# Split products with the weights' low part last, states in 2 KB runs, and small conversions on ScalarE, in a one-core decoder step

## The chip, the cores and the metric

The kernel runs on one core of a Trainium2 chip. The metric is the time of one execution on the device in microseconds, the median over several runs. Besides, one execution was recorded by the hardware profiler; its rows carry the names of the engines: PE (TensorE, matrix products), PEld (its weight loads), DVE (VectorE), ACT (ScalarE), POOL (GpSimd) and SP (SyncE, which here only issues DMAs). "SPq" and "ACTq" are the instructions that issue DMAs on those queues.

## The reference

One layer of a decoder, in float32, for 1024 prompt tokens and 64 sample tokens (8 sequences of 8), width 1024. Cut to what matters:

```python
xn = rmsnorm(h, norm_mix)
proj = xn @ w_in                      # 2048 columns for retention, 1792 for RWKV-7
# retention, 8 heads of 64: q, k with rope, state S (64 x 64) per sequence and head, chunks of 128
o_ret = head_norm(retention(q, k, v, s_ret)) * silu(g_ret)
# RWKV-7, 8 heads of 64: f mixes each row with the row before it (token shift)
f = rw_p + (prev - rw_p) * rw_mu
o_rw = (head_norm(rwkv7_scan(r, log_w, k7, kk, a, v7, s_wkv)) ... ) * gate
h = h + concat([o_ret, o_rw]) @ w_out
# PEER: product keys, 8 heads x 2 x 128 keys, 16 of 16384 experts for each head and token
s = einsum(xb @ wq, keys); sv, si = top_k(s, 16)
cand = sv[:, :, 0, :, None] + sv[:, :, 1, None, :]; cv, ci = top_k(cand, 16)
e = si0[ci // 16] * 128 + si1[ci % 16]
act = gelu(einsum('pd,phkd->phk', xb, u_tab[e])) * softmax(cv)
h = h + einsum('phk,phkd->pd', act, v_tab[e])
h = h + sigmoid(rmsnorm(h, ple_norm) @ ple_gate) * (p_l @ ple_proj)
y = rmsnorm(h, norm_final)
```

Returned besides `y` are the new states of both mixers for the prompt and for each of the 8 sequences of the sample group, and the last projected rows.

## The kernel before

Tokens are tiled by 128: tiles 0 to 7 are the prompt, tile 8 holds the 64 sample tokens.

**Split products.** A product that needs more than one pass's precision is made from two parts of each operand. `split` (L296) has ACT copy the source into the high part (type float32r), and DVE or POOL subtract that from the source for the low part. `mm3` (L324) then adds three products for each step k of the contraction: high by high, high by low, low by high. It is called for the projections (`a_ret`, L361, with the tokens as the stationary operand and the weights `wh`, `wl` moving; `a_rw`, L519, with the weights stationary), for the queries (`c_query`, L1006), for `hidden` (L1259, the weights `uh`, `ul` stationary, eight steps) and for `ple` (L1376, the tokens stationary). `dense` (L1288) has the same three products written out, for blocks b of 128 experts: `vh` by `ah`, `vh` by `al`, `vl` by `ah`.

**Stages.** In order of time:

1. Projections (`group_a`, three groups of tiles: 0 and 1, 2 and 3, 4 to 8). Results go to DRAM: `rd` for retention and `fd` for RWKV. `fd` is one tensor of 128 partitions x 14 x 1088 tokens; `a_rw` writes one of the 14 rows for all tokens of its group at a time (L559), on ACT's queue.
2. Mixers (`group_b`, L648), tile by tile in the order 1, 8, 2 to 7. `rw_mix` loads its tile's part of `fd` into `ft` (L708, one buffer). Tile 8 reads and writes the states of the eight sequences: `seq_state` (L422) for both mixers, L489 and L493 for retention, L947 and L955 for RWKV. In DRAM a state is laid out sequence, head, row, column, so that each of 64 partitions takes eight pieces of 64 values. Behind the mixers run `c_rows` (the output projection, with its weights `cw` loaded on SP's queue) and the expert search and gathers of tiles 0, 1 and 8 (`early`, L1214).
3. Queries and first top 16 of the tiles 2 to 7 (`c_query`, `pick`).
4. `topk` (L1041) for tiles 4 to 7 (group `G2`) and 2 and 3 (`G1`), the gates of G2 (`gates`, L1230: one-hot matrices, scaled by ACT at L1247, multiplied on PE), and `hidden` for the first 96 blocks of 128 experts, whose results are stored in DRAM (`gd`).
5. For G2 all 16384 experts are computed densely: `dense_fused` (L1310) for the last 32 blocks, in groups of four, with `hidden` for the next group between; then `dense_stored` (L1329) for the 96 stored blocks in groups of five. For each group `act` (L1273) makes `ah` and `al` from eight buffers (`AB`); then for each of eight slices d of the width, `dense` loads `vraw`, splits it (`vh` on ACT, `vl` on POOL, two buffers each), runs the products of the group into one PSUM tile `py`, and adds that to `yT` on DVE (L1307).
6. `ple`: the last gate, the final norm and the output.

**Gathers.** For G1 the experts are fetched row by row (`gather`, L1120): POOL issues an indirect DMA of 128 rows of 4 KB (L1130) into one of five buffers, and DVE multiplies and sums each (L1144 for `u`, L1158 for `v`). They run beside stages 4 and 5, on the same POOL and DVE queues as the splits of the weights and the sums into `yT`.

**Order.** Each engine runs its instructions in one fixed order. The kernel is built with `TileContext(nc, schedule_with_timeline_sim=True)`: the order in each queue is planned when the program is built, from a simulated time line, not taken as written. Waits follow from the tiles' readers and writers and from their buffers.

**Conversions.** In `topk`, DVE turns the found indices from integers to floats (L1053) and scales half of them by 128 (L1054), turns the second search's indices into floats (L1079), and for G2 the two halves of the expert's number (L1118). In `gates`, DVE copies the transposed softmax out of PSUM (L1237).

Of the kernel before, what the change touches and what calls it, by code (L numbers as in the profile page):

```python
# [8 lines left out]
F32 = mybir.dt.float32  # L9
# [4 lines left out]
AF = mybir.ActivationFunctionType  # L14
# [10 lines left out]
RW = 1792  # L25
# [89 lines left out]
def pack(i):  # L115
    f = lambda a: np.asarray(a)
    w_in = f(i['w_in'])[0]
    r = {}
    r['x'] = np.concatenate([f(i['x_prompt'])[0], f(i['x_sample']).reshape(64, D)], 0)
    r['w_ret'] = w_in[:, :RET].reshape(8, 128, 8, 256).transpose(2, 1, 0, 3)  # L120
    r['w_rw'] = w_in[:, RET:].reshape(8, 128, 14, 128).transpose(2, 1, 0, 3)
    r['w_out'] = f(i['w_out'])[0].reshape(8, 128, 1024)
    col = lambda a, n: a.reshape(n, 128).T
    r['vec'] = np.concatenate([col(f(i['rw_mu'])[0], 14), col(f(i['rw_kk'])[0], 4), col(f(i['rw_ka'])[0], 4),
                               col(f(i['rw_rk'])[0].reshape(512), 4), col(f(i['rw_a0'])[0], 4)], 1)
    r['w2aug'] = np.concatenate([f(i['rw_w2'])[0], f(i['rw_w0'])], 0)
    r['a2'] = f(i['rw_a2'])[0]
    r['g2'] = f(i['rw_g2'])[0]
    r['rows'] = np.concatenate([f(i['norm_mix'])[0], f(i['norm_ffn'])[0], f(i['ple_norm'])[0], f(i['norm_final']),
                                f(i['rw_ln_g'])[0], f(i['rw_ln_b'])[0]])  # L130
    r['s_ret'] = f(i['state_ret'])[0]
    r['s_wkvT'] = f(i['state_wkv'])[0].transpose(0, 1, 3, 2)
    r['shiftT'] = f(i['state_shift'])[0].reshape(8, 14, 128).transpose(2, 1, 0)
    r['cst'] = consts()
    r['rope'] = ropes()
    r['wq'] = f(i['peer_wq'])[0].reshape(8, 128, 16, 128).transpose(2, 1, 0, 3)
    r['keysT'] = f(i['peer_keys'])[0].reshape(16, 128, 128).transpose(2, 0, 1)
    r['pu'] = f(i['peer_u'])[0]
    r['puT'] = r['pu'].reshape(128, 128, 8, 128).transpose(0, 3, 2, 1)
    r['pv'] = f(i['peer_v'])[0]  # L140
    r['pvd'] = r['pv'].reshape(128, 128, 8, 128).transpose(2, 1, 0, 3)
    p = np.concatenate([f(i['p_prompt'])[0, 0], f(i['p_sample'])[0].reshape(64, 256)], 0)
    r['pT'] = p.T.reshape(2, 128, T).transpose(1, 0, 2)
    r['pgate'] = f(i['ple_gate'])[0].reshape(8, 128, 1024)
    r['pproj'] = f(i['ple_proj'])[0].reshape(2, 128, 1024)
    return {k: np.ascontiguousarray(v) for k, v in r.items()}


OUTS = {'y': ((T, D), 'float32'), 'ret_p': ((8, 64, 64), 'float32'), 'wkv_p': ((8, 64, 64), 'float32'),
        'shift': ((9, RW), 'float32'), 'ret_s': ((8, 8, 64, 64), 'float32'), 'wkv_s': ((8, 8, 64, 64), 'float32')}  # L150
ROWS = {'norm_mix': (0, 1024), 'norm_ffn': (1024, 1024), 'ple_norm': (2048, 1024), 'norm_final': (3072, 1024),
# [3 lines left out]
def unpack(r):  # L155
    return (r['y'][:SEQ].reshape(1, SEQ, D), r['y'][SEQ:].reshape(8, 8, D),
            r['ret_p'].reshape(1, 1, 8, 64, 64), r['wkv_p'].reshape(1, 1, 8, 64, 64), r['shift'][:1].reshape(1, 1, RW),
            r['ret_s'].reshape(1, 8, 8, 64, 64), r['wkv_s'].reshape(1, 8, 8, 64, 64), r['shift'][1:].reshape(1, 8, RW))

# [53 lines left out]
class K:  # L213
# [28 lines left out]
    def setup(self):  # L242
        nc = self.nc
        rp = self.pool("root")
        self.dp = self.pool("dscr", space=bass.MemoryType.DRAM)
        self.csta = rp.tile([128, CSTA], F32, name="csta")
        nc.sync.dma_start(self.csta, self.I['cst'][:, :CSTA])
        self.hp = rp.tile([128, 8], F32, name="halves")
        nc.vector.memset(self.hp, -0.5)
        self.eid = {t: rp.tile([128, 64 if t == 8 else 128], I32, name=f"eid{t}") for t in E0 + G1}  # L250
        self.gsm = {t: rp.tile([128, 64 if t == 8 else 128], F32, name=f"gsm{t}") for t in E0 + G1}
        self.hd = {t: self.dp.tile([128, D], F32, name=f"hd{t}") for t in range(9)}
        self.xd = {t: self.dp.tile([128, D], F32, name=f"xd{t}") for t in range(9)}
        self.od = {t: self.dp.tile([128, D], F32, name=f"od{t}") for t in range(9)}
        self.yd = {t: self.dp.tile([128, D], F32, name=f"yd{t}") for t in range(9)}
        self.fd = self.dp.tile([128, 14, T], F32, name="fd")
        self.sd = {t: self.dp.tile([128, 16, 128], F32, name=f"sd{t}") for t in range(9)}
        self.rd = {t: self.dp.tile([128, RET], F32, name=f"rd{t}") for t in range(9)}
# [64 lines left out]

    def mm3(self, out, lh, ll, rh, rl, nk, first=True, last=True):  # L324
        mm = self.nc.tensor.matmul
        for k in range(nk):
            mm(out, lh(k), rh(k), start=first and k == 0, stop=False)  # L327
            mm(out, lh(k), rl(k), start=False, stop=False)  # L328
            mm(out, ll(k), rh(k), start=False, stop=last and k == nk - 1)  # L329

# [30 lines left out]
    def a_ret(self, wp, tiles, x, ready, tags):  # L361
        nc, I = self.nc, self.I
        off, _ = spans(tiles)
        if True:
            for cb in range(8):
# [10 lines left out]
                for t in tiles:  # L376
# [3 lines left out]
                    self.mm3(p[:n, :256], lambda k: x[0][:, k, o:o + n], lambda k: x[1][:, k, o:o + n],  # L380
                             lambda k: wh[k // 4][:, k % 4, :], lambda k: wl[k // 4][:, k % 4, :], 8)
                    d = wp.tile([128, 256], F32, name="retd", bufs=4)
# [39 lines left out]
    def seq_state(self, wp, src, st, hp):  # L422

        nc = self.nc
        sr = wp.tile([128, 8, 64], F32, name="sr", tag="x2k", bufs=CRING)
        for s in range(2):
            nc.sync.dma_start(sr[64 * s:64 * s + 64], st[:, 2 * hp + s].rearrange("b j i -> j b i"))
        return wp, src, sr
# [9 lines left out]
    def ret_mix(self, wp, t):  # L438
# [41 lines left out]
        if smp:  # L480
            stk = self.c("seqtok", 64)
            for h in range(8):
# [5 lines left out]
                s0 = self.co.tile([64, 8, 64], F32, name="sr0", tag="x2k", bufs=4)  # L488
                nc.sync.dma_start(s0, I['s_ret'][:, h].rearrange("b d v -> d b v"))  # L489
                sn = self.co.tile([64, 8, 64], F32, name="srn", tag="x2k", bufs=4)  # L490
                nc.vector.tensor_tensor(sn, p[:64].rearrange("p (b d) -> p b d", b=8), s0, op=OP.add)
                nc.vector.tensor_scalar(sn, sn, self.c("gc8", 64)[:, h:h + 1], None, op0=OP.mult)
                nc.scalar.dma_start(O['ret_s'][:, h].rearrange("b d v -> d b v"), sn)  # L493
                yield
# [24 lines left out]
    def a_rw(self, wp, tiles, x, tags):  # L519
# [6 lines left out]
        for i, ft in enumerate((12, 13, 4, 5, 6, 7, 0, 1, 2, 3, 8, 9, 10, 11)):  # L526
# [27 lines left out]
            if smp:  # L554
# [3 lines left out]
                nc.vector.tensor_copy(self.shl[:, 1:9, ft], rs[:, :, 8])  # L558
            nc.scalar.dma_start(self.fd[:, ft, t0:t0 + ntok], dst)  # L559
        if smp:  # L560
# [135 lines left out]
    def rw_mix(self, t):  # L696
# [10 lines left out]
        ft = wp.tile([128, 14, n], F32, name="ft")  # L707
        nc.sync.dma_start(ft, self.fd[:, :, o:o + n])  # L708
        rT, kT, vT = ft[:, 0:4, :n], ft[:, 4:8, :n], ft[:, 8:12, :n]
# [222 lines left out]
        else:  # L932
# [6 lines left out]
            for h in range(8):  # L939
# [6 lines left out]
                s0 = self.co.tile([64, 8, 64], F32, name="sw0", tag="x2k", bufs=4)  # L946
                nc.sync.dma_start(s0, I['s_wkvT'][:, h].rearrange("b j i -> j b i"))  # L947
                nc.vector.tensor_tensor(s0, p[:64].rearrange("p (b d) -> p b d", b=8), s0, op=OP.add)
# [5 lines left out]
                nc.scalar.activation(s1, p2[:64], AF.Copy)  # L954
                nc.scalar.dma_start(O['wkv_s'][:, h].rearrange("b i j -> i b j"), s1)  # L955
                yield
# [84 lines left out]
    def topk(self, tp, t, s=None, tags={}, ce=None):  # L1041
# [10 lines left out]
        sf = tp.tile([128, 8, 2, 16], F32, name="sf")  # L1052
        nc.vector.tensor_copy(sf[:n].rearrange("p h c k -> p (h c) k"), si[:n])  # L1053
        nc.vector.tensor_scalar(sf[:n, :, 0], sf[:n, :, 0], 128.0, None, op0=OP.mult)  # L1054
        svv = sv.rearrange("p (h c) k -> p h c k", c=2)
# [22 lines left out]
        cf = tp.tile([128, 128], F32, name="cf")  # L1078
        nc.vector.tensor_copy(cf[:n], ci[:n].rearrange("p h k -> p (h k)"))  # L1079
        ef = tp.tile([128, 128], F32, name="ef")  # L1080
# [31 lines left out]
        else:  # L1112
# [4 lines left out]
            nc.vector.tensor_scalar(e1[:n, 1], ei[:n], 127, None, op0=OP.bitwise_and)  # L1117
            nc.vector.tensor_copy(self.e12[t][:n], e1[:n])  # L1118

# [110 lines left out]
    def gates(self, wp, t):  # L1230
# [5 lines left out]
        it = wp.tile([128, 128], F32, name="it", bufs=2)  # L1236
        nc.vector.tensor_copy(it[:, :n], p[:, 2, :n])  # L1237
        io = self.c("iota")[:, None, :].to_broadcast([128, 4, 128])
# [49 lines left out]
    def dense(self, dl, dr, yT, groups, acts_of, side):  # L1288
        nc, I = self.nc, self.I
        for g0, nb in groups:  # L1290
            acts = acts_of(g0, nb)
            for d in range(8):
# [6 lines left out]
                p = self.ps2.tile([128, self.ntok], F32, name="py")  # L1299
                for b in range(nb):  # L1300
                    ah, al = acts[b]
                    for j, (lh, rh) in enumerate(((vh, ah), (vh, al), (vl, ah))):
                        nc.tensor.matmul(p, lh[:, b, :], rh, start=b == 0 and j == 0, stop=b == nb - 1 and j == 2)  # L1303
                if self.first:
# [253 lines left out]
```

## Time and profile before

| | |
|---|---|
| median of 3 runs | 3877.64 us (3877.34 to 3881.52) |
| profiled execution, its own time | 3881.51 us |
| its span, first to last instruction | 3879.7 us |
| mean granted clock of PE | 0.883 |
| PE busy | 3346.4 us (86%) |
| DVE busy | 2984.9 us (77%) |
| POOL busy | 2361.5 us (61%) |
| ACT busy | 1220.5 us (31%) |
| moved by DMA | 1086.23 MB, mean 280 GB/s |

The span is the profiled execution's time but for 1.8 us around it. A busy time is a sum over the whole span; the stages differ much, so that no share of the table is the share of a stage. A row of a group names the line, the engine, the operation and the tiles written and read; a row of a wait names who waited, who ended the wait, the total in us, how often, and the longest one.

### The profile page before, as it was taken

What the parts mean: (1) busy time and instruction counts of PE and PEld (TensorE: products, weight loads), DVE (VectorE), ACT (ScalarE), POOL (GpSimd) and SP (SyncE); (2) the same over time, 40 slices, a digit from 0 to 9 for tenths busy, and PEclk for the clock granted to TensorE, in tenths of its full rate; (3) what the DMA queues carried; (4) which work ended last, traced back from release to release, by engine and by line L of the source; (5) the groups of instructions that cost most, each with busy time, mean ns of one, the idle gap of its engine ahead of it and who ended that gap; (6) DMA issues with size and microseconds to landing.
All of it is one profiled execution on the core that took longest, in us unless ns stands there. A gap on an engine that the chain in (4) does not pass through costs nothing.

```text
span 3879.7 us, 52665 instructions
## 1 busy us (share of the span) xinstructions
PE 3346.4 (86%) x17749; PEld 2748.3 (71%) x17749; DVE 2984.9 (77%) x5884; ACT 1220.5 (31%) x2247; POOL 2361.5 (61%) x2059
## 2 busy tenths in 40 slices
PE   7789995868779878883999989999899989899979
PEld 7688894645747757662887767887688766677757
DVE  4454388877787697876998999977777777788875
ACT  4232220111111111211232626777533333333322
POOL 5363176454365365554569888875688787777740
PEclk9799995667868567876999999999899999999989
DMA  7266558899778878889779888998999999999962
GB/s 249 74 218 208 172 179 285 279 300 296 231 243 285 294 264 272 290 288 327 223 261 309 298 289 316 315 349 320 346 339 339 336 361 359 358 352 345 334 223 72
DMA packets 457320, 1086.23 MB, mean 280 GB/s; under 512 B 73627, under 2 KB 176281, under 8 KB 452378
## 3 DMA queue, kind: packets, MB, share of 16 engines
q0 software_dynamic: 165888, 604.05, 44.4%
q1 hardware_dynamic: 236638, 382.77, 31.0%
q10 hardware_dynamic: 54524, 96.03, 6.6%
q8 instruction: 141, 2.31, 0.2%
q14 instruction: 129, 1.06, 0.1%
HBM read 986.68 MB, written 95.94 MB: 279 GB/s over the span
## 4 chain that ended last, share of the span: by engine, by line
PE 37%; DVE 24%; DMA 12%; POOL 8%; issue 8%; ACT 3%; ACTq 0%; SPq 0%; POOLq 0%; DVEq 0%
PE py L1303 13%; DVE grow L1144 6%; POOL grow L1130 4%; DMA grow<-in_pu,eid 4%; DVE gacc L1158 3%; DMA grow<-in_pv,eid 3%; PE ph L327 2%; PE ph L329 2%; PE ph L328 2%; POOL vl L302 2%; PE epq L1198 2%; DMA ft<-fd 2%; DVE eq L1085 2%; PE ewo L612 2%; DVE oh L1245 1%
## 5 line engine op out<-in xcount | busy, mean ns | idle before, releaser
L1130 POOL DMA_INDIRECT grow<-in_pv,eid x576 | 572.0, 993 | 497.4 <-DVE gacc L1158 310.2
L1130 POOL DMA_INDIRECT grow<-in_pu,eid x576 | 573.3, 995 | 432.5 <-DVE grow L1144 257.9
L1158 DVE SCALAR_TENSOR_TENSOR gacc<-grow,ac,gacc 128x1024 f32<-128x1024 f32 x571 | 732.2, 1282 | 51.1 <-DMA grow<-in_pv,eid 46.3
L1144 DVE SCALAR_TENSOR_TENSOR grow<-grow,gacc 128x1024 f32<-128x1024 f32 x576 | 690.3, 1213 | 87.8 <-DMA grow<-in_pu,eid 77.2
L1303 PE MATMUL py<-ah,vl 128*128 128x512 f32 x1024 | 410.0, 403 | 40.6 <-POOL vl L302 40.0
L1303 PE MATMUL py<-ah,vh 128*128 128x512 f32 x1024 | 406.9, 398 | 16.1 <-ACT vh L298 9.5
L329 PE MATMUL ph<-cx,ul 128*128 128x512 f32 x1024 | 406.5, 398 | 14.4 <-POOL ul L302 14.3
L327 PE MATMUL ph<-cx,uh 128*128 128x512 f32 x1024 | 408.6, 399 | 5.4 <-ACT uh L298 3.6
L328 PE MATMUL ph<-cx,uh 128*128 128x512 f32 x1024 | 406.2, 397 | 0.0
L1303 PE MATMUL py<-al,vh 128*128 128x512 f32 x1024 | 405.0, 396 | 0.0
L302 POOL TENSOR_TENSOR vl<-vraw,vh 128x640 fp32r<-128x640 f32 (+2 forms) x224 | 325.5, 1457 | 33.3 <-ACT vh L298 29.6
L302 POOL TENSOR_TENSOR ul<-uraw,uh 128x1024 fp32r<-128x1024 f32 x128 | 308.0, 2406 | 53.5 <-ACT uh L298 50.9
L1303 PEld LDWEIGHTS py<-ah,vl 128*128 128x128 f32 x1024 | 193.4, 189 | 108.0 <-POOL vl L302 67.0
L298 ACT ACTIVATE vh<-vraw 128x640 fp32r<-128x640 f32 (+2 forms) x224 | 154.5, 692 | 356.4 <-PE py L1303 173.8
L1307 DVE TENSOR_TENSOR yT<-yT,py 128x512 f32<-128x512 f32 x216 | 147.7, 685 | 127.7 <-PE py L1303 126.9
L1303 PEld LDWEIGHTS py<-ah,vh 128*128 128x128 f32 x1024 | 194.5, 190 | 69.2 <-ACT vh L298 21.9
L329 PEld LDWEIGHTS ph<-cx,ul 128*128 128x128 f32 x1024 | 194.7, 190 | 60.6 <-POOL ul L302 20.9
L327 PEld LDWEIGHTS ph<-cx,uh 128*128 128x128 f32 x1024 | 194.9, 190 | 46.7 <-ACT uh L298 5.3
L298 ACT ACTIVATE uh<-uraw 128x1024 fp32r<-128x1024 f32 x128 | 135.2, 1057 | 286.9 <-DMA uraw<-in_puT 144.3
L1303 PEld LDWEIGHTS py<-al,vh 128*128 128x128 f32 x1024 | 193.8, 189 | 44.2
L328 PEld LDWEIGHTS ph<-cx,uh 128*128 128x128 f32 x1024 | 195.3, 191 | 39.3
L1245 DVE TENSOR_TENSOR oh<-csta,pit 128x512 f32<-128x512 f32 x256 | 162.3, 679 | 43.1 <-PE pwt L1250 42.9
(400 smaller groups left out, 7806.7 us busy)
## 6 DMA issues: line engine op xcount, KB each, us to landing
uraw<-in_puT SPq DMA_DIRECT2D x128, 512.0 KB, 4.7
vraw<-in_pvd SPq DMA_DIRECT2D x152, 320.0 KB, 5.9
cw<-in_w_out SPq DMA_DIRECT2D x128, 256.0 KB, 5.2
wd<-wst ACTq DMA_DIRECT2D x28, 1024.0 KB, 15.2
wt<-wd SPq DMA_DIRECT2D x64, 448.0 KB, 7.6
wraw<-in_w_ret SPq DMA_DIRECT2D x48, 512.0 KB, 4.9
ewq<-in_wq SPq DMA_DIRECT2D x48, 512.0 KB, 5.1
gd<-geh ACTq DMA_DIRECT2D x96, 256.0 KB, 5.2
```

The lines of the kernel that those rows point to most:

```text
L298: nc.scalar.activation(hi, src, AF.Copy)
L302: nc.gpsimd.tensor_tensor(lo, src, hi.bitcast(F32), op=OP.subtract)
L327: mm(out, lh(k), rh(k), start=first and k == 0, stop=False)
L328: mm(out, lh(k), rl(k), start=False, stop=False)
L329: mm(out, ll(k), rh(k), start=False, stop=last and k == nk - 1)
L612: nc.tensor.matmul(p[:n], oT[k // 4][:, k % 4, :n], w, start=k == 0, stop=k == 7)
L1130: nc.gpsimd.indirect_dma_start(out=g, out_offset=None, in_=src, in_offset=bass.IndirectOffsetOnAxis(ap=self.eid[t][:, j:j + 1], axis=0))
L1144: nc.vector.scalar_tensor_tensor(g[:, c], g[:, c], 1.0, x[:, c], op0=OP.mult, op1=OP.mult, accum_out=hv[:, i, j:j + 1])
L1158: nc.vector.scalar_tensor_tensor(y[:, c], g[:, c], ac[:, j:j + 1], y[:, c], op0=OP.mult, op1=OP.add)
L1245: nc.vector.tensor_tensor(oh[j], io, p[:, j, s + b:s + b + 4, None].to_broadcast([128, 4, 128]), op=OP.is_equal)
L1303: nc.tensor.matmul(p, lh[:, b, :], rh, start=b == 0 and j == 0, stop=b == nb - 1 and j == 2)
L1307: nc.vector.tensor_tensor(yT[:, d, :], yT[:, d, :], p, op=OP.add)
```

## The change

Five edits. The computation stays the same; sums are added in another order.

- In `mm3` and in `dense`, the products of a group that use the low part of the stationary operand come after all others, in a second loop. `a_ret`, where the weights are the moving operand, passes `right=True`, which puts the products with the moving operand's low part last instead. `ple` doesn't pass it.
- The states of the sample group lie in DRAM as head, row, sequence, column, in the inputs and the outputs, so that a partition's eight pieces are one run of 2 KB instead of eight of 256 bytes. The host turns them before and after.
- `fd` lies as tile, partition, row, token, so that a tile's load is one run of 7 KB in each partition. The stores are cut at tiles into runs of 512 bytes, and the sample tokens get a store of their own.
- In `topk`, for the tiles 2 to 7, the conversion of the indices (L1053 and L1054 become two instructions), of the second search's indices (L1079), and of the halves (L1118) go to ACT.
- In `gates`, the copy L1237 goes to ACT.

```diff
-        self.fd = self.dp.tile([128, 14, T], F32, name="fd")
+        self.fd = self.dp.tile([9, 128, 14, 128], F32, name="fd")
...
-    def mm3(self, out, lh, ll, rh, rl, nk, first=True, last=True):
+    def mm3(self, out, lh, ll, rh, rl, nk, first=True, last=True, right=False):
         mm = self.nc.tensor.matmul
         for k in range(nk):
             mm(out, lh(k), rh(k), start=first and k == 0, stop=False)
-            mm(out, lh(k), rl(k), start=False, stop=False)
-            mm(out, ll(k), rh(k), start=False, stop=last and k == nk - 1)
+            mm(out, *((ll(k), rh(k)) if right else (lh(k), rl(k))), start=False, stop=False)
+        for k in range(nk):
+            mm(out, *((lh(k), rl(k)) if right else (ll(k), rh(k))), start=False, stop=last and k == nk - 1)
...
-            nc.sync.dma_start(sr[64 * s:64 * s + 64], st[:, 2 * hp + s].rearrange("b j i -> j b i"))
+            nc.sync.dma_start(sr[64 * s:64 * s + 64], st[2 * hp + s])
...
-                nc.sync.dma_start(s0, I['s_ret'][:, h].rearrange("b d v -> d b v"))
+                nc.sync.dma_start(s0, I['s_ret'][h])
...
-                nc.scalar.dma_start(O['ret_s'][:, h].rearrange("b d v -> d b v"), sn)
+                nc.scalar.dma_start(O['ret_s'][h], sn)
...
-            nc.scalar.dma_start(self.fd[:, ft, t0:t0 + ntok], dst)
+            nc.scalar.dma_start(self.fd[t0 // 128:(t0 + np_) // 128, :, ft].rearrange("t p n -> p t n"), dst[:, :np_].rearrange("p (t n) -> p t n", n=128))
+            if smp:
+                nc.scalar.dma_start(self.fd[8, :, ft, :64], dst[:, np_:])
...
-        nc.sync.dma_start(ft, self.fd[:, :, o:o + n])
+        nc.sync.dma_start(ft, self.fd[t, :, :, :n])
...
-                nc.sync.dma_start(s0, I['s_wkvT'][:, h].rearrange("b j i -> j b i"))
+                nc.sync.dma_start(s0, I['s_wkvT'][h])
...
-                nc.scalar.dma_start(O['wkv_s'][:, h].rearrange("b i j -> i b j"), s1)
+                nc.scalar.dma_start(O['wkv_s'][h], s1)
...
-        nc.vector.tensor_copy(sf[:n].rearrange("p h c k -> p (h c) k"), si[:n])
-        nc.vector.tensor_scalar(sf[:n, :, 0], sf[:n, :, 0], 128.0, None, op0=OP.mult)
+        if t in G1 + G2:
+            sr = si[:n].rearrange("p (h c) k -> p h c k", c=2)
+            for c in range(2):
+                nc.scalar.activation(sf[:n, :, c], sr[:, :, c], AF.Copy, scale=(128.0, 1.0)[c])
+        else:
+            nc.vector.tensor_copy(sf[:n].rearrange("p h c k -> p (h c) k"), si[:n])
+            nc.vector.tensor_scalar(sf[:n, :, 0], sf[:n, :, 0], 128.0, None, op0=OP.mult)
...
-        nc.vector.tensor_copy(cf[:n], ci[:n].rearrange("p h k -> p (h k)"))
+        if t in G1 + G2:
+            nc.scalar.activation(cf[:n], ci[:n].rearrange("p h k -> p (h k)"), AF.Copy)
+        else:
+            nc.vector.tensor_copy(cf[:n], ci[:n].rearrange("p h k -> p (h k)"))
...
-            nc.vector.tensor_copy(self.e12[t][:n], e1[:n])
+            nc.scalar.activation(self.e12[t][:n], e1[:n], AF.Copy)
...
-        nc.vector.tensor_copy(it[:, :n], p[:, 2, :n])
+        nc.scalar.activation(it[:, :n], p[:, 2, :n], AF.Copy)
...
-                for b in range(nb):
-                    ah, al = acts[b]
-                    for j, (lh, rh) in enumerate(((vh, ah), (vh, al), (vl, ah))):
-                        nc.tensor.matmul(p, lh[:, b, :], rh, start=b == 0 and j == 0, stop=b == nb - 1 and j == 2)
+                for b, (ah, al) in enumerate(acts[:nb]):
+                    nc.tensor.matmul(p, vh[:, b, :], ah, start=b == 0, stop=False)
+                    nc.tensor.matmul(p, vh[:, b, :], al, start=False, stop=False)
+                for b, (ah, al) in enumerate(acts[:nb]):
+                    nc.tensor.matmul(p, vl[:, b, :], ah, start=False, stop=b == nb - 1)
```

More of the change, by code (lines that the diff above doesn't have):

```diff
@@ L130, in pack @@
                                 f(i['rw_ln_g'])[0], f(i['rw_ln_b'])[0]])
-    r['s_ret'] = f(i['state_ret'])[0]
-    r['s_wkvT'] = f(i['state_wkv'])[0].transpose(0, 1, 3, 2)
+    r['s_ret'] = f(i['state_ret'])[0].transpose(1, 2, 0, 3)
+    r['s_wkvT'] = f(i['state_wkv'])[0].transpose(1, 3, 0, 2)
     r['shiftT'] = f(i['state_shift'])[0].reshape(8, 14, 128).transpose(2, 1, 0)
@@ L149 @@
 OUTS = {'y': ((T, D), 'float32'), 'ret_p': ((8, 64, 64), 'float32'), 'wkv_p': ((8, 64, 64), 'float32'),
-        'shift': ((9, RW), 'float32'), 'ret_s': ((8, 8, 64, 64), 'float32'), 'wkv_s': ((8, 8, 64, 64), 'float32')}
+        'shift': ((9, RW), 'float32'), 'ret_s': ((8, 64, 8, 64), 'float32'), 'wkv_s': ((8, 64, 8, 64), 'float32')}
 ROWS = {'norm_mix': (0, 1024), 'norm_ffn': (1024, 1024), 'ple_norm': (2048, 1024), 'norm_final': (3072, 1024),
@@ L157, in unpack @@
             r['ret_p'].reshape(1, 1, 8, 64, 64), r['wkv_p'].reshape(1, 1, 8, 64, 64), r['shift'][:1].reshape(1, 1, RW),
-            r['ret_s'].reshape(1, 8, 8, 64, 64), r['wkv_s'].reshape(1, 8, 8, 64, 64), r['shift'][1:].reshape(1, 8, RW))
+            r['ret_s'].transpose(2, 0, 1, 3).reshape(1, 8, 8, 64, 64), r['wkv_s'].transpose(2, 0, 1, 3).reshape(1, 8, 8, 64, 64), r['shift'][1:].reshape(1, 8, RW))
 CSTA = 256
@@ L380, in a_ret @@
                     self.mm3(p[:n, :256], lambda k: x[0][:, k, o:o + n], lambda k: x[1][:, k, o:o + n],
-                             lambda k: wh[k // 4][:, k % 4, :], lambda k: wl[k // 4][:, k % 4, :], 8)
+                             lambda k: wh[k // 4][:, k % 4, :], lambda k: wl[k // 4][:, k % 4, :], 8, right=True)
                     d = wp.tile([128, 256], F32, name="retd", bufs=4)
```

## The prediction

> **What bounds the kernel now.** First the page: its span and the lines of the chain that ended last.
>
> ```profile
> span 3879.7 us, 52665 instructions
> PE py L1303 13%; DVE grow L1144 6%; POOL grow L1130 4%; DMA grow<-in_pu,eid 4%; DVE gacc L1158 3%; DMA grow<-in_pv,eid 3%; PE ph L327 2%; PE ph L329 2%; PE ph L328 2%; POOL vl L302 2%; PE epq L1198 2%; DMA ft<-fd 2%; DVE eq L1085 2%; PE ewo L612 2%; DVE oh L1245 1%
> ```
>
> No line has more than 13%, so there is no single bound, and each edit must be priced in its own stage. I cut the span where the code changes stage: projections, mixers with the early gathers behind them, queries, gates with `hidden`, `dense_fused`, and `dense_stored` in two pieces. Columns: stretch, length, busy time (and instructions) of PE, its weight loads, DVE, ACT and POOL, granted clock, DMA share, GB/s.
>
> ```profile
> 0.00:600.00 600.00, 514.72 (x3928) 491.14 (x3928) 312.67 (x685) 174.83 (x306) 272.56 (x257) 0.93 0.58 188
> 600.00:1780.00 1180.00, 911.91 (x4965) 710.43 (x4965) 955.77 (x1833) 173.09 (x375) 603.80 (x594) 0.71 0.84 278
> 1780.00:2010.00 230.00, 195.72 (x1095) 164.92 (x1096) 202.54 (x825) 63.64 (x103) 121.32 (x97) 0.91 0.76 252
> 2010.00:2760.00 750.00, 687.11 (x3362) 568.91 (x3361) 663.49 (x1320) 442.65 (x861) 583.22 (x434) 0.97 0.91 317
> 2760.00:3050.00 290.00, 290.00 (x1265) 237.26 (x1265) 225.20 (x256) 87.83 (x133) 242.32 (x199) 1.00 0.95 334
> 3050.00:3430.00 380.00, 336.29 (x1364) 255.81 (x1363) 292.76 (x529) 135.02 (x225) 296.21 (x249) 0.98 1.00 356
> 3430.00:3700.00 270.00, 265.66 (x1122) 207.93 (x1120) 222.12 (x297) 97.75 (x161) 206.73 (x172) 1.00 0.98 342
> ```
>
> PE is busy without a break in 2760 to 3050, so nothing in that stretch can gain from an earlier operand. In 3050 to 3430 PE idles 380 - 336 = 44 us while the DMA share is 1.00. In 2010 to 2760 DVE (88%) and PE (92%) are close together. From 600 to 1780 no compute engine is full (DVE 81%).
>
> Next, who PE waits for in `dense_stored`: engine and line, awaited, us in total, times, longest. The first four rows are from 3060 to 3430, the last two from 3430 to 3700.
>
> ```profile
> PEld py L1303 <- POOL vl L302: 58.3, 47, 2.7
> PE py L1303 <- POOL vl L302: 37.7, 41, 2.2
> DVE yT L1307 <- PE py L1303: 73.5, 53, 4.5
> ACT ah L298 <- PE py L1303: 31.8, 10, 4.6
> ...
> PEld py L1303 <- POOL vl L302: 8.5, 16, 1.3
> ACT ah L298 <- PE py L1303: 10.8, 5, 3.1
> ```
>
> POOL makes the low part `vl` late, PE stops on it, and DVE then stops on PE. These are the waits that the reordering aims at.
>
> **The change part by part.** I take gains off the profiled execution, which was timed at 3881.5 us around its 3879.7 us span; the median of the three runs is 3877.6, or 3.9 lower, and the same gains come off that.
>
> *Dense products.* The chain gives the spacing of matmuls that nothing holds up, and the tile's rows the cost of `vl`:
>
> ```profile
> 2823.85 5.53 PE py L1303 x24
> ...
> L302 POOL TENSOR_TENSOR vl<-vraw,vh x89: 1273/1573/1600, 3059.4 to 3428.0; 128x640 fp32r<-128x640 f32 x79, 128x512 fp32r<-128x512 f32 x10
> ```
>
> 5.53 / 24 = 0.23 us per matmul. With five blocks in a group, the first product with `vl` moves from third to eleventh place, so `vl` may come 8 x 0.23 = 1.84 us later. The mean wait was 58.3 / 47 = 1.24 us, the longest 2.7: most would vanish if everything else stayed in time. So the term lies between nothing and 58.3 us, and 37.7 of it is time in which PE itself idled. But the stretch's DMA share is already 1.00. Its fastest 50 us were
>
> ```profile
> 3150.00:3200.00 50.00, 43.51 (x181) 32.86 (x180) 38.36 (x69) 17.12 (x28) 40.90 (x35) 1.00 1.03 372
> ```
>
> and if the same bytes must flow at 372 instead of 356 GB/s at best, the 380 us shrink by 380 x (1 - 356/372) = 16 us. After that the gathers' arrival is late next, and DVE waits for it in the place of PE. I take 15 us, next to this cap, and 3 of the 8.5 us in 3430 to 3700.
>
> The Trainium skill, page "DMA: Bandwidth & Descriptors", section "Specifications", gives about 358 GB/s as one core's share of HBM; by it this term would be about 2 us. The row of 372 is already above that figure, so it isn't a hard wall here, and my cap stands on the row.
>
> The same reordering frees `ah` later. Eight buffers serve groups of five, so the fourth `ah` of a group takes the buffer of the first of the group before. In that group's last pass (d = 7) its last reader was the third matmul of 15 and becomes the eleventh. The next group reads its fourth `ah` after six matmuls instead of nine. From release to need there were (15-3)+9 = 21 matmuls, 4.83 us; there will be (15-11)+6 = 10, 2.30 us. In between lie
>
> ```profile
> L298 ACT ACTIVATE ah<-ph x128: 577/597/603, 2754.0 to 3672.1; 128x512 fp32r<-128x512 f32 x128
> L300 DVE TENSOR_TENSOR al<-ph,ah x128: 681/684/693, 2755.4 to 3673.6; 128x512 fp32r<-128x512 f32 x128
> ```
>
> 0.60 + 0.68 = 1.28 us, plus whatever is queued ahead on ACT and DVE. The cover falls from 3.5 to 1.0 us, in 19 groups. The price is between 0 and 19 x 1.84 = 35 us; I take 5 us lost, near the low end because 1.28 fits into 2.30.
>
> *`mm3`.* In `hidden`, of eight steps, `ul` is needed after 16 products instead of two, 14 x 0.23 = 3.2 us later. From 2010 to 2700, and for `wl` over the projections:
>
> ```profile
> PEld ph L329 <- POOL ul L302: 20.9, 16, 3.8
> PE ph L329 <- POOL ul L302: 14.3, 13, 3.4
> ...
>   PE pret L328: 5.5, 4
>   PE prw L329: 5.1, 3
> ```
>
> `hidden` can gain between 0 and 20.9 us; DVE is nearly as full as PE there, so I take 8. The projections can gain between 0 and 10.6 us; PE is the fullest engine (86%), so I take 5. In `ple` the stationary operand is the state, so its low part moves last, not the weights'; the weights were split long before, and I take 0.
>
> *Runs of states and of `fd`.* Median us from issue to landing, the last column:
>
> ```profile
> ft<-fd SPq DMA_DIRECT2D x8, 896.0 KB, 9.7
> qv<-rd SPq DMA_DIRECT2D x8, 1024.0 KB, 9.3
> rope<-in_rope SPq DMA_DIRECT2D x36, 128.0 KB, 4.6
> sr<-in_s_wkvT SPq DMA_DIRECT2D x16, 128.0 KB, 11.2
> ...
>   ACT tw L712: 58.7, 9
> ...
> 849.86 12.05 SPq L427 DMA_DIRECT2D sr<-in_s_wkvT  x6
> 862.01 11.25 DMA cw<-in_w_out
> 357.10 0.33 SPq L385 DMA_DIRECT2D rope<-in_rope  x1
> ```
>
> `ft` is read in 512-byte runs and will be one 7 KB run for each partition. `qv` has 8 KB runs already: scaled by bytes, 9.3 x 896/1024 = 8.1 us against 9.7. That is 1.6 us for each of nine loads, 14 us; ACT waits for all nine, and the chain holds most of them. Against it the writes of `fd` get 512-byte runs, and the last group 14 more issues (0.33 us each on ACT, which is 29% busy in that stage). Ends -3 and +14; I take 8. The state transfers (56 of 128 KB, in 256-byte runs) become 2 KB runs like those of other loads. On SP six of them held the queue for 12.05 us, and behind them stood the `cw` load that is on the chain. Six issues like `rope`'s take 6 x 0.33 = 2 us, so `cw` could start up to 10 us sooner; the other 50 are seldom waited for. Between 0 and 12 us; I take 8.
>
> *Conversions.* Off DVE:
>
> ```profile
> L1053 DVE CAST sf<-si x9: 267/285/2402, 483.1 to 2406.8; 128x256 f32<-128x256 uint32 x8, 64x256 f32<-64x256 uint32 x1
> L1054 DVE TENSOR_SCALAR sf<-sf x9: 195/218/502, 484.7 to 2411.8; 128x128 f32<-128x128 f32 x8, 64x128 f32<-64x128 f32 x1
> L1079 DVE CAST cf<-ci x9: 209/222/2272, 490.9 to 2480.3; 128x128 f32<-128x128 uint32 x8, 64x128 f32<-64x128 uint32 x1
> L1118 DVE CAST e<-e x4: 295/350/387, 2135.2 to 2489.0; 128x256 f32<-128x256 int32 x4
> L1237 DVE COPY it<-pit x4: 270/276/294, 2142.6 to 2658.9; 128x128 f32<-128x128 f32 x4
> L1202 ACT ACTIVATE es<-epq x48: 257/277/278, 391.8 to 1328.5; 128x128 f32<-128x128 f32 x32, 64x128 f32<-64x128 f32 x16
> ```
>
> Six tiles x (0.285 + 0.218 + 0.222) and four x (0.350 + 0.276) are 6.9 us. On ACT it is 6 x 3 + 4 x 3 pieces of 128 columns at 0.277 us, 8.3 us; ACT is 59% busy there. New is a round trip: `cf` waits in ACT's queue behind gate scalings, `eq` on DVE waits for `cf`, and the gathers' sums stand behind `eq`. Ends -5 and +6.9; I take 2. The Trainium skill, page "ScalarE: Activation LUTs", section "Rules for kernel authors", says to put plain arithmetic on VectorE and not on ScalarE. By it this term would be a loss of 8.3 - 6.9 = 1.4 us; the rows agree that ACT is dearer for each piece, but ACT has the room and DVE hasn't.
>
> **Sum.** 15 + 3 - 5 + 8 + 5 + 8 + 8 + 2 = 44 us. 3881.5 - 44 = 3837.5 for the profiled execution, 3877.6 - 44 = 3834 for the median.
>
> **The rivals.**
>
> *The stored dense stage doesn't move.* DMA is full there, and PE's waits only turn into waits for gathers. For it: shares of 1.00 and 0.98. Against it: the 372 row. The dense terms (15 + 3 - 5) go and 31 us remain: 3847.
>
> *All waits for low parts vanish.* 37.7 us of PE's idle time in the dense stage, 14.3 in `hidden`, 10.6 in the projections, with 18 from the other terms: 81 us, 3797. For it: PE idle under these names. Against it: the DMA share.
>
> *Slower: the `ah` buffers.* ACT takes its work in order, so a later `ah` holds back the `vh` splits behind it, POOL's `vl` comes later by as much, and the delay is paid twice: 19 x 2 x 1.84 = 70 us. The other terms give 49, so 3877.6 + 21 = 3899. It decides from 49 / 19 = 2.6 us lost in each group. For it: ACT already waits 31.8 + 10.8 us for these buffers, 15 times. Against it: no row shows PE waiting for a late `al`.
>
> **How the numbers follow.** My forecast has 0.42, the unmoved dense stage 0.25, the vanished waits 0.15, the `ah` buffers 0.18. About 0.2% (7.8 us) is what a measurement of this kernel can tell from no change. Faster: nearly all of the first three, 0.76; within it, their tails and a mild form of the last, 0.08; slower 0.16. The order in each queue is planned when the program is built, so a shifted need can move other work too. The range 3788 to 3888 takes in the first three cases with their unknown ends and the milder half of the last.
>
> **What would show it.** Right: PE's wait for `vl` in the stored dense stage falls from 58.3 us to under 20, DMA share stays near 1.00, DVE's waits for gathers grow, and that stage is about 13 us shorter; `ft` lands in about 8 us; SP's burst of six state loads takes under 5 us; ACT's wait for `ah` grows by less than 2 us a group. Wrong: PE waits for `ah` or `al` at the start of each group of five; or the waits for `vl` are gone and the stage keeps its 650 us; or the mixers' stage changes by more than 25 us either way, which none of my terms explains.

## The result and the profile after

The changed kernel takes 3813.9 us (median of four runs, 3809.5 to 3819.1) against 3878.6 us (3877.3 to 3881.5) beside it: ratio 0.9829, 95% interval 0.9812 to 0.9846, or 65 us faster. The forecast was 44 us faster. When the pair ran again among the experiments below, it gave 3824.9 against 3879.6: 0.9860 (0.9836 to 0.9884), 55 us. One run of the kernel before among the experiments took 7342 us and is left out of every ratio and range.

The stages can be cut at the same instructions in both profiles. These rows give, for a tile, its first and last start; before, then after:

```profile
L327 PE MATMUL prw<-x,wh x448: 276/292/579, 69.1 to 589.7; 128*128 128x256 f32 x75, 128*128 128x288 f32 x75
L327 PE MATMUL pq<-cx,wqh x256: 277/387/776, 1812.8 to 1992.6; 128*128 128x256 f32 x64, 128*128 128x512 f32 x64
L327 PE MATMUL ph<-cx,uh x1024: 387/389/774, 1995.8 to 3065.3; 128*128 128x512 f32 x171
L1303 PE MATMUL py<-ah,vh x1024: 387/389/793, 2754.7 to 3705.2; 128*128 128x512 f32 x171
```

```profile
span 3809.0 us, 52675 instructions
...
L327 PE MATMUL prw<-x,wh x448: 276/293/580, 70.5 to 579.5; 128*128 128x256 f32 x75, 128*128 128x288 f32 x75
L327 PE MATMUL pq<-cx,wqh x256: 277/387/796, 1756.8 to 1935.5; 128*128 128x256 f32 x64, 128*128 128x512 f32 x64
L327 PE MATMUL ph<-cx,uh x1024: 387/389/796, 1939.7 to 3016.5; 128*128 128x512 f32 x171
L1312 PE MATMUL py<-ah,vh x1024: 387/389/797, 2707.0 to 3638.3; 128*128 128x512 f32 x171
```

| stage | from, to | before | after | change | forecast |
|---|---|---|---|---|---|
| projections | 0, last `prw` | 589.7 | 579.5 | -10.2 | -5 |
| mixers | last `prw`, first `pq` | 1223.1 | 1177.3 | -45.8 | -16 |
| queries | first `pq`, first `ph` | 183.0 | 182.9 | -0.1 | 0 |
| gates and `hidden` | first `ph`, first `py` | 758.9 | 767.3 | +8.4 | -10 |
| `dense_fused` | first `py`, last `ph` | 310.6 | 309.5 | -1.1 | 0 |
| `dense_stored` | last `ph`, last `py` | 639.9 | 621.8 | -18.1 | -13 |
| `ple` | last `py`, end | 174.5 | 170.7 | -3.8 | 0 |

The chain of waits on the page after reaches back over less than a tenth of the span, so the two chains can't be compared. Two stages are not where the forecast put them: the mixers gained three times as much, and gates and `hidden` got longer. In the stored dense stage the windows answer to those of before (length, PE, weight loads, DVE, ACT, POOL, clock, DMA share, GB/s):

```profile
3008.00:3370.00 362.00, 328.70 (x1369) 259.73 (x1367) 289.18 (x524) 135.38 (x225) 291.93 (x246) 0.98 1.02 368
3370.00:3640.00 270.00, 259.38 (x1111) 207.55 (x1109) 221.48 (x298) 96.15 (x162) 208.17 (x176) 0.99 0.96 342
...
3150.00:3200.00 50.00, 44.28 (x186) 34.65 (x185) 41.10 (x77) 18.90 (x31) 41.43 (x35) 0.98 1.05 380
```

The first piece is 18 us shorter for nearly the same number of matmuls (1364 and 1369), at 368 instead of 356 GB/s. The waits after, from 3010 to 3370, against two rows of before, from 3060 to 3430, of ACT's wait for `vraw` and PE's for `vh`:

```profile
ACT vh L298 <- DMA vraw<-in_pvd: 68.1, 25, 6.2
...
DVE yT L1319 <- PE py L1315: 49.1, 41, 2.9
ACT ah L298 <- PE py L1315: 30.0, 8, 5.8
...
PEld py L1312 <- ACT vh L298: 24.4, 12, 3.9
...
PEld py L1315 <- POOL vl L302: 19.3, 17, 3.3
```

```profile
ACT vh L298 <- DMA vraw<-in_pvd: 18.5, 6, 5.0
...
PEld py L1303 <- ACT vh L298: 10.7, 12, 1.6
```

PE's weight loads wait 19.3 us for `vl` instead of 58.3. What is late next is DMA, but not through the gathers: the load of `vraw` arrives late for `vh` (68.1 us, 25 times, instead of 18.5 and 6), and PE then waits for `vh` (24.4 us instead of 10.7).

### The profile page after: what moved, and what is told of

Read it like the earlier page. It is cut to its first block, busy times and chain, and to the rows that moved or that the text cites. A ratio compares the mean times of both kernels' runs of the same rounds, so it can differ in the third digit from the quotient of the medians.

```text
span 3809.0 us, 52675 instructions
## 1 busy us (share of the span) xinstructions
PE 3309.1 (87%) x17749; PEld 2745.7 (72%) x17749; DVE 2966.1 (78%) x5858; ACT 1228.1 (32%) x2273; POOL 2368.8 (62%) x2059
## 5 line engine op out<-in xcount | busy, mean ns | idle before, releaser
L1315 PE MATMUL py<-ah,vl 128*128 128x512 f32 x1024 | 275.5, 400 | 16.7 <-POOL vl L302 15.6
L330 PE MATMUL ph<-cx,ul 128*128 128x512 f32 x1024 | 260.3, 393 | 6.0 <-POOL ul L302 6.0
L327 PEld LDWEIGHTS ph<-cx,uh 128*128 128x128 f32 x1024 | 196.5, 192 | 58.3 <-ACT uh L298 8.8
L1256 DVE TENSOR_TENSOR oh<-csta,pit 128x512 f32<-128x512 f32 x256 | 161.3, 679 | 49.3 <-PE pwt L1261 42.6
```

The costliest lines, as they stand in the source:

```text
L330: mm(out, *((lh(k), rl(k)) if right else (ll(k), rh(k))), start=False, stop=last and k == nk - 1)
L1256: nc.vector.tensor_tensor(oh[j], io, p[:, j, s + b:s + b + 4, None].to_broadcast([128, 4, 128]), op=OP.is_equal)
L1315: nc.tensor.matmul(p, vl[:, b, :], ah, start=False, stop=b == nb - 1)
```

## The experiments

They ran in three sets, each on another chip and each with runs of the kernel before beside it: `e1_products`, `e2_layout`, `e3_conv` and `a_noconv`; then `after_again`, `swap_old`, `e6_dense` and `e7_mm3`; then `swap_e2_old`, `swap_b_new`, `e8_hidden` and `a_oldhidden`. The 74 runs of the kernel before spread from 3857 to 3898 us, so ratios are given with their 95% intervals, always to the kernel before of the same set. Kernels of different sets are compared by these ratios. A stage of a single profile is less sure still, which the next kernel shows.

### The changed kernel again (`after_again`)

> The changed kernel once more, on the chip of the runs beside it. Theory G (a part of the mixers' 46 us is the granted clock, 0.70 before and 0.72 after: PE was busy 928 us before and 905 us after for the same 5013 and 5018 matmuls): the ratio comes nearer to that without the conversions, 0.986 to 0.990, and a profile at a clock of 0.70 to 0.71 shows mixers 10 to 30 us longer than 1177. Theories T (transfers) and P (planned order): the ratio stays at 0.983, the mixers within 5 us of 1177.

3824.9 us, 0.9860 (0.9836 to 0.9884). In its profile (span 3836.3 us) the mixers took 1192.5 us, cut as above, where the first profile had 1177.3. Two kernels below (`a_noconv`, `a_oldhidden`) have the same order of instructions on PE and DVE until past the mixers, and the same transfers: 1209.7 and 1185.2. The mean of the four is 1191. Four kernels whose mixers are those of before (before, `e3_conv`, `e6_dense`, `e8_hidden`) took 1223.1, 1225.2, 1213.0 and 1213.9, mean 1219. So the mixers gained about 28 us by one profile of each kernel, and the 45.8 of the first pair of profiles were partly chance. Theory G, that the granted clock makes the spread, fits loosely: PE's busy time for the same matmuls was 905 us in the shortest stage and 936 in the longest, but 929 in the one of 1185.

### The parts alone (`e1_products`, `e2_layout`, `e3_conv`) and all but the conversions (`a_noconv`)

Each is the kernel before with some of the change's hunks: `mm3` with `right=True` and the dense loop (e1); the layouts of `fd` and of the states (e2); `topk` and `gates` (e3). `a_noconv` has all but the last.

> The kernel before with only the products reordered (mm3 and dense); layouts and conversions as before. Theory A (each edit acts in its own stage): the projections end about 10 us sooner, stored dense is about 18 us shorter, the mixers keep their 1223 us within 5: ratio about 0.992 (30 us). Theory B (the 46 us of the mixers come from the transfers of fd and the states): the same as A here, with the mixers unmoved. Theory C (the mixers' gain is the order that is planned anew for any edit, whatever the edit is): the mixers move by more than 10 us here too, though no product in them is changed.

> The kernel before with only the layouts of fd and of the states changed. Theory A (terms as forecast): 16 us in all, ratio about 0.996, and the mixers' stage 16 us shorter. Theory B (the transfers themselves are worth all that the mixers gained): the mixers' stage 40 to 50 us shorter, ratio about 0.988, stored dense unchanged within 5 us. Theory C (a new order): the mixers move by an amount that the shorter waits for ft and sr (14 us and 10 us at most) don't account for.

> The kernel before with only the small conversions moved from DVE to ACT. Theory A (own stage): between 2 us faster and 5 us slower, ratio 0.9995 to 1.0013, all of it in queries, gates and hidden. Theory B: the same. Rival for the 8 us by which queries, gates and hidden got longer in the changed kernel: the conversions' round trip over ACT costs it, then this run is 8 us slower, ratio 1.002. Theory C: the mixers, before which nothing is changed, move by more than 10 us.

> The changed kernel with the conversions back on DVE. If the edits add up, its distance from the changed kernel is that of the conversions alone taken the other way, within 5 us, so about 3812 us (ratio to before 0.983). If the conversions are what made queries, gates and hidden 8 us longer, it is the faster one, 3806 us. If a new order moves the mixers as much as an edit does, they differ from the changed kernel's 1177 us by more than 10 us.

| kernel | median us | ratio (95%) | gates and `hidden` |
|---|---|---|---|
| `e1_products` | 3872.0 | 0.9973 (0.9946 to 1.0000) | 785.9 |
| `e2_layout` | 3880.5 | 0.9998 (0.9975 to 1.0021) | 780.6 |
| `e3_conv` | 3877.4 | 0.9992 (0.9973 to 1.0012) | 765.1 |
| `a_noconv` | 3834.4 | 0.9882 (0.9847 to 0.9917) | 788.4 |

The sum of the three parts is 14 us, the whole is worth 55. In e1 and e2 the time before the queries got shorter (projections and mixers 33 and 20 us less than before), and gates and `hidden`, in which e2 changes nothing, gave 27 and 22 us back. Either the parts need each other, or the order that is planned anew for each kernel costs as much as the part brings. The next three kernels tell these apart.

### One plan, other transfers (`swap_old`, `swap_e2_old`, `swap_b_new`)

The order of every queue is planned as for the named kernel; then, after planning, only the access patterns of the DMAs of `fd` and the states are replaced (the same values move, and the host's layout follows). From the new runs to the old ones, for the states:

```diff
-    ap=[[512, 64], [1, 512]], offset=h * 32768
+    ap=[[64, 64], [32768, 8], [1, 64]], offset=h * 4096
```

`fd` likewise gets rows of 1152 tokens, its loads runs of 512 bytes, and its stores one run in each partition. `swap_old` has the plan of the changed kernel and the runs of before, `swap_e2_old` the plan of `e2_layout` and the runs of before, `swap_b_new` the plan of before and the states (not `fd`) in 2 KB runs.

> The changed kernel with its own planned order of every queue, but the transfers of fd and of the states in the old runs (512 bytes and 256 bytes): after the plan is made, the access patterns of these DMAs are put back. Theory T (the runs themselves shorten the mixers): it loses the mixers' gain, 30 to 46 us slower than the changed kernel, ratio to before about 0.992 to 0.996. Theory P (the order that was planned with the shorter transfers is what gains): within 10 us of the changed kernel. My terms alone (16 us for both layouts) would have it 16 us slower than the changed kernel.

> The kernel with only the layouts changed, which took as long as before (ratio 0.9998), in its own planned order, with the transfers of fd and of the states put back into the old runs. Under the changed kernel's plan the runs alone were worth 16 us (3840.7 against 3824.9). Theory T (the runs are worth that much under any plan, and here the plan ate it): 16 us slower than before, ratio 1.004. Rival (under this plan the transfers are hidden and worth nothing): ratio 1.000.

> The kernel before in its own planned order of every queue, with only the transfers of the states put into 2 KB runs after the plan is made; fd stays as it was. My term for the states is 8 us, between 0 and 12: ratio 0.998. If the 16 us that the runs are worth under the changed kernel's plan come from fd alone: ratio 1.000. SP's burst of six state loads, 12.05 us before, takes under 5 us in any case.

`swap_old`: 3840.7, 0.9892 (0.9867 to 0.9917), 16 us slower than the changed kernel by the medians and 12 by the ratios; the two intervals overlap, so this pair alone is not clear of noise. `swap_e2_old`: 3898.1, 1.0054 (1.0025 to 1.0083); with the new runs the same plan had 0.9998 (0.9975 to 1.0021), so they are worth 0.0056 x 3878 = 22 us there, and the intervals don't overlap. `swap_b_new`: 3872.5, 0.9995 (0.9971 to 1.0020), 2 us, between 8 slower and 11 faster.

So the runs are worth 12 to 22 us under either plan; my two terms together said 16. And `swap_e2_old` differs from before in hardly more than its order (the 14 extra stores of the sample tokens remain, and `fd`'s rows are 1152 tokens apart instead of 1088): that order alone costs 21 us (10 to 32), and it hid what the layouts bring in `e2_layout`. Theory T is right about the transfers, but its 30 to 46 us are two to three times too large; theory P, as a gain, is not borne out in the one profile of `swap_old`, whose mixers (1216 us) are those of before.

Which transfer it is, the waits and the landing times of `after_again` and then `swap_old` say:

```profile
ACT tw L715 <- DMA ft<-fd: 35.9, 7, 10.9
```

```profile
ft<-fd SPq DMA_DIRECT2D x8, 896.0 KB, 7.2
sr<-in_s_wkvT SPq DMA_DIRECT2D x16, 128.0 KB, 5.9
```

```profile
ACT tw L715 <- DMA ft<-fd: 58.7, 9, 13.2
```

```profile
ft<-fd SPq DMA_DIRECT2D x8, 896.0 KB, 11.9
sr<-in_s_wkvT SPq DMA_DIRECT2D x16, 128.0 KB, 14.4
```

ACT's wait for `ft` is 22.8 us shorter (33.9 us between `swap_e2_old` and `e2_layout`, 79.0 and 45.1), and this load stands on the chain of before. The RWKV states land 8.5 us sooner each, and the waits for the states fall as well: PE waits twice in `swap_old`, 8.0 us in all, and DVE four times, 10.8 us; in `after_again` DVE alone waits, twice, 3.5 us. How the gain divides between `fd` and the states these waits don't decide. In `swap_b_new` SP's burst and the load behind it, and what SP waited for between 850 and 890:

```profile
856.39 4.24 SPq L427 DMA_DIRECT2D sr<-in_s_wkvT  x6
868.96 11.98 SPq L611 DMA_DIRECT2D cw<-in_w_out  x4
```

```profile
SPq L611 <- PE pX L436: 8.7, 3, 4.8
```

The burst takes 4.24 us instead of 12.05 (5.55 in the changed kernel, where I had said under 5), but `cw` starts 14.6 us after the burst's first issues (at 854.36) where it started 16.7 after them before: its buffer is set free by PE, not by the burst.

### The products, where the plan ahead of them stays (`e6_dense`, `e8_hidden`) and where it doesn't (`e7_mm3`, `a_oldhidden`)

`e6_dense` is before with the dense loop alone, `e7_mm3` before with `mm3` and `right=True` alone, `e8_hidden` before with the second loop in `hidden` alone, and `a_oldhidden` the changed kernel with the old order in `hidden`. The edit of `e8_hidden`, with the call of `mm3` written out (`a_oldhidden` has it the other way round):

```diff
 for k in range(8):
     nc.tensor.matmul(p, uh[:, k, :], x[0][:, k], start=k == 0, stop=False)
     nc.tensor.matmul(p, uh[:, k, :], x[1][:, k], start=False, stop=False)
+for k in range(8):
     nc.tensor.matmul(p, ul[:, k, :], x[0][:, k], start=False, stop=k == 7)
```

> The kernel before with only the dense products reordered. In this kernel the planned order stays as before up to the queries, so mixers and projections are a control. Theory A (own stage): stored dense 15 to 20 us shorter, ratio 0.995 to 0.996. My rival of the full DMA: stored dense unmoved, ratio 1.000. Theory G: the mixers move with the granted clock although nothing in them is changed, by about as much as PE's busy time in them.

> The kernel before with only the order of the products in mm3 changed (projections, queries, hidden). As forecast: projections 5 and hidden 8 us shorter, 13 in all, ratio 0.9966. By the stages of the changed kernel: projections 10 us shorter, queries, gates and hidden not shorter, ratio 0.997 to 0.998. Theory P: the mixers, whose order is planned anew here too, move by 10 us or more at the same granted clock.

> The kernel before with only the products in hidden reordered; the planned order stays as before up to the queries. My term: 8 us faster, ratio 0.998, PE's waits for ul (14.3 and 20.9 us) halved. Rival from the run with mm3 alone, whose gates and hidden took 27 us more: the plan puts the gelus of hidden earlier into ACT's queue, where they wait for PE and hold back the gate scalings behind them; then gates and hidden take 780 us or more and the ratio is 1.003 to 1.006, with ACT's wait of the gelus for PE at 30 to 40 us instead of 4.7.

> The changed kernel with the products of hidden in the old order. If the reordering is worth the 8 us of my term there: ratio 0.988, 8 us slower than the changed kernel's 0.986. If it is worth nothing: 0.986. If it costs (gates and hidden are 8 us longer in the changed kernel than before): 0.984, and gates and hidden back at 760 us.

| kernel | median us | ratio (95%) | gates and `hidden` | `dense_stored` |
|---|---|---|---|---|
| `e6_dense` | 3862.3 | 0.9951 (0.9932 to 0.9971) | 759.8 | 622.6 |
| `e8_hidden` | 3866.0 | 0.9969 (0.9950 to 0.9988) | 749.5 | 639.9 |
| `e7_mm3` | 3881.6 | 1.0013 (0.9992 to 1.0035) | 786.5 | 639.8 |
| `a_oldhidden` | 3834.0 | 0.9891 (0.9863 to 0.9919) | 764.8 | 636.7 |

With the plan ahead untouched each product edit acts in its own stage alone: the dense loop takes 17 us off stored dense and leaves gates and `hidden` at 759.8 (before 758.9); `hidden` takes 9 us off its stage and leaves stored dense at 639.9. By the ratios they are worth 19 and 12 us (17 and 11 by the medians). For the dense loop there is a second pair: `e1_products` is `e7_mm3` with this loop besides, and its ratio is lower by 0.0040, 16 us (2 to 29), with stored dense at 626.9 instead of 639.8. PE's wait for `vl` over the whole of stored dense in before (3057 to 3706) and then in `e6_dense` (3055 to 3678):

```profile
PEld py L1303 <- POOL vl L302: 67.0, 64, 2.7
```

```profile
PEld py L1304 <- POOL vl L302: 25.7, 31, 1.8
```

The other kernels make the gain of that stage smaller than 17 us. In seven profiles with the new dense loop it takes 621.8 to 636.7 us, mean 627.4, in seven without it 634.8 to 639.9, mean 637.9: 10.5 us.

PE's waits for `ul`, 20.9 and 14.3 us before, in `e8_hidden`:

```profile
PEld ph L1272 <- POOL ul L302: 10.7, 8, 2.7
PE ph L1272 <- POOL ul L302: 7.5, 6, 2.3
```

`e7_mm3` shortens the projections to 575.1 and then loses 27 us in gates and `hidden`. Windows and ACT's wait of the gelus for PE, in that stage of before and then of `e7_mm3`:

```profile
1996.00:2755.00 759.00, 696.32 (x3414) 577.05 (x3412) 672.52 (x1389) 446.62 (x866) 586.74 (x435) 0.97 0.90 315
```

```profile
ACT geh L1270 <- PE ph L329: 4.7, 4, 1.9
```

```profile
1980.00:2767.00 787.00, 704.08 (x3417) 588.77 (x3416) 686.99 (x1404) 448.46 (x866) 590.56 (x440) 0.95 0.87 307
```

```profile
ACT geh L1271 <- PE ph L330: 36.5, 13, 7.7
```

PE has the same matmuls; ACT now stands 36.5 us before gelus whose products are not ready, with the gate scalings queued behind, and DVE has 15 more instructions in the stage. The granted clock is lower as well (0.95 instead of 0.97), but PE's busy time, 7.8 us longer, covers no more than a part of the 28 us. `e2_layout` (40.6 us), `swap_e2_old` (36.7) and `e1_products` (38.3) show the same wait and 777 to 786 us. It is a mark of these plans rather than the whole cause: `a_noconv` has 788.4 us without it (7.5), and `a_oldhidden` 764.8 with it (32.4). Why these plans cost some 20 us there stays open.

`a_oldhidden` is 12 us slower than the changed kernel by the ratios, but the intervals overlap, and in its profile gates and `hidden` are no longer than in the changed kernel's two (764.8 against 767.3 and 769.4), while stored dense is (636.7 against 621.8 and 629.7): what the new order in `hidden` is worth inside the changed kernel stays open.

## Why the prediction held, and where its sizes were off

| term | forecast | measured | by |
|---|---|---|---|
| dense products | 15 + 3 - 5 = 13 | 19 (11 to 26) | `e6_dense` |
| the same, in its stage | 13 | 10.5 | `dense_stored`: mean 627.4 of seven profiles with the new loop, 637.9 of seven without |
| `hidden` | 8 | 12 (5 to 19) | `e8_hidden`, plan of before ahead |
| projections | 5 | 12 | end of the projections: mean 576.9 of seven profiles with `mm3` changed, 588.5 of seven without |
| runs of `fd` and states | 8 + 8 = 16 | 12 to 16, and 22 | `swap_old`, `swap_e2_old` |
| conversions | 2 | 3 (-5 to 10) | `e3_conv` |

With the first row of the dense products these sum to about 62 us, and the change brought 55 and 65. The terms are real, but that the total came out near the forecast is partly luck, because misses in the stages cancel: the mixers gained 28 us (46 in the first profile) instead of 16 and the projections 12 instead of 5, while gates and `hidden` got 8 us longer instead of 10 shorter.

- **Dense products.** The mechanism held: `vl` is no longer what PE waits for, and DMA is the next limit. The cap of 16 us stood on a best window of 372 GB/s; the changed kernel reached 380 in one, so that this was no wall. Whether the term was too small stays open: the whole kernel says 19 us, the stage 10.5 on average. The forecast that DVE would wait for gathers was wrong; `vraw` is late instead. The loss for `ah` shows. These are rows of stored dense in before (3057 to 3706), and then after (3008 to 3640):

```profile
ACT ah L298 <- PE py L1303: 42.6, 15, 4.6
```

```profile
ACT ah L298 <- PE py L1315: 56.4, 16, 5.8
...
ACT ah L298 <- PE py L1313: 6.5, 2, 4.7
PEld py L1313 <- DVE al L300: 5.5, 7, 1.2
...
PEld py L1312 <- ACT ah L298: 2.2, 5, 1.4
```

  ACT waits 62.9 us for the buffers instead of 42.6, 1.1 us more a group, and the rival that needed 2.6 doesn't hold here. PE's weight loads now wait 12 times for a late `al` or `ah`, 7.7 us in all (PE's matmuls 3.8 us), where before has no such row. The prediction had named waits of this kind at every group as a mark of being wrong; they come in a mild form, of the size of the 5 us that it took off.
- **Projections.** The bound of 10.6 us counted only the waits named after `wl`; the measured 12 us lie slightly above it, and what the rest was I have not traced. PE's 86% in that stage was the reason to take 5, and it did not hold the gain down.
- **States and `fd`.** The sum was near, the split isn't shown: `fd` wasn't run alone. Under the plan of before the states were worth about 2 us (8 slower to 11 faster) instead of 8. The reason given for the 8, `cw` up to 10 us sooner, brought 2, since `cw` then waited for its buffer. For `fd` the scaling by bytes from `qv` held: in `after_again` `qv` lands in 8.3 us, and 8.3 x 896/1024 = 7.3 against 7.2 for `ft`. The size it was set against did not: in 512-byte runs `ft` landed in 9.7 us in before but in 11.9 under the changed kernel's plan, so that under one plan the loads landed 4.7 us apart and not 1.6.
- **Conversions.** On ACT, in gates and `hidden` of the changed kernel, they take 7.8 us (forecast 8.3):

```profile
L1059 ACT ACTIVATE sf<-si 128x128 f32<-128x128 uint32 x12 | 3.1, 298 | 15.2 <-DVE si L1042 13.2 <-POOL eid L1076 2.0
L1088 ACT ACTIVATE cf<-ci 128x128 f32<-128x128 uint32 x6 | 1.9, 311 | 12.8 <-DVE eq L1096 8.7 <-DVE ci L1084 4.1
...
L1129 ACT ACTIVATE e<-e 128x256 f32<-128x256 int32 x4 | 1.7, 413 | 7.2 <-DVE e L1128 7.2
...
L1248 ACT ACTIVATE it<-pit 128x128 f32<-128x128 f32 x4 | 1.1, 287 | 0.0
```

  But DVE is rid of more than 6.9. In the same stage before:

```profile
L1079 DVE CAST cf<-ci 128x128 f32<-128x128 uint32 x6 | 5.9, 985 | 0.0
L1053 DVE CAST sf<-si 128x256 f32<-128x256 uint32 x6 | 4.8, 794 | 0.0
L1054 DVE TENSOR_SCALAR sf<-sf 128x128 f32<-128x128 f32 x6 | 1.6, 266 | 0.0
L1118 DVE CAST e<-e 128x256 f32<-128x256 int32 x4 | 1.4, 346 | 0.1
L1237 DVE COPY it<-pit 128x128 f32<-128x128 f32 x4 | 1.1, 279 | 1.5 <-PE pit L1235 1.5
```

  These are 14.8 us, because the sum was made with medians (0.222 us for `cf`) where the mean is 0.985. Of the 7.9 us more than forecast little reached the end of `e3_conv`; inside the changed kernel the difference (0.9882 without, 0.9860 with) is 8.5 us, with overlapping intervals.
- **Gates and `hidden`** were to be 10 us shorter and are 8 longer. The terms are real (`e8_hidden`), but the plan of this kernel takes them back: with the old order in `hidden` the stage is as long (764.8).
- **The mark of a wrong prediction**, a mixers' stage that moves by over 25 us, was met: by 46 us in the first profile and by about 28 over four. The runs explain 12 to 22 of these; the rest stays open. SP's burst, at 5.55 us, also missed its mark of under 5.

## What to carry to other kernels

When the order of a kernel's queues is planned at build time, an edit's own worth and the worth of the order that it triggers are of one size here (20 us): put the edit in after the plan, or choose one that leaves the plan ahead of it alone, before calling it useless. Price an operation with its mean in the stage, not its median. Of the transfers that get faster, price those for which an engine with nothing else to do is waiting: in `swap_b_new` SP's burst of state loads became 8 us shorter, and the load behind it started 2 us sooner.

## What the runs showed of the hardware that was not expected

The long casts on DVE have a cause that the trace shows. DVE's and then POOL's rows before:

```profile
2043.33 2.27 DVE L1079 CAST cf<-ci 128x128 f32<-128x128 uint32 x1
...
2406.78 2.40 DVE L1053 CAST sf<-si 128x256 f32<-128x256 uint32 x1
```

```profile
2043.10 2.40 POOL L302 TENSOR_TENSOR ul<-uraw,uh 128x1024 fp32r<-128x1024 f32 x1
...
2406.62 2.40 POOL L302 TENSOR_TENSOR ul<-uraw,uh 128x1024 fp32r<-128x1024 f32 x1
```

Each cast began while POOL subtracted and ended 0.10 and 0.16 us after it (2045.60 and 2045.50, 2409.18 and 2409.02): a cast of 0.22 or 0.29 us stood out the subtraction. Of the 18 conversions `sf` and `cf` that DVE made in that stage of before, nine met a two-input instruction of POOL, and all nine ended 0.09 to 0.16 us after it; the other nine took 0.20 to 0.29 us. The Trainium skill, page "SBUF — State Buffer", section "SBUF: two separate sides", says that DVE and GpSimd share a pair of ports, which one instruction holds to its end while the other is blocked; these rows agree. On ACT, in `e3_conv`, the `cf` conversion took 0.30 to 0.33 us each time.

The Trainium skill's 358 GB/s for a core's share of HBM (page "DMA: Bandwidth & Descriptors", section "Specifications") was passed again: 368 over 362 us, 380 in 50.
